# A re-planned head of an RMS norm and QKV projection: first tile cast and transposed in bfloat16, fourth tile loaded sooner, a crossbar transpose moved ahead of a weight piece

## The chip, the cores and the metric

One core of one Trainium2 chip. The metric is the device time of one execution in microseconds (us). "Span" is the time from the first to the last instruction of the profiled program; it is some 2 us shorter than the time. The calls ran on different chips, and each call ran the kernel before beside the others, so a ratio compares runs of one call.

## The reference

```python
batch, n_heads, seq, head_dim = 8, 12, 1024, 64          # x is 8192 x 768, w_qkv 768 x 2304
rms = np.sqrt(np.mean(x ** 2, axis=-1, keepdims=True) + eps)
x_norm = x / rms * gamma
return np.matmul(x_norm, w_qkv).astype(np.float32)
```

## The kernel before

64 row tiles of 128 rows. A tile is loaded in float32, turned into bfloat16 and transposed so that the 768 columns lie on the partitions (`xT`), and multiplied with `gamma * w_qkv` in bfloat16 (`w_b`). The row's 1/rms is applied as the product leaves PSUM. From the seventh tile on everything follows one regular loop. The first six tiles, the head, run while the weights arrive in pieces; there each operation stands in a hand-made list with a time that only sets the order of emission.

```python
HEAD = 6
def load_x(t):   X[t] = xin.tile(...);  nc.sync.dma_start(out=X[t], in_=xf[t*P:(t+1)*P, :])
def load_w(c):   # a float32 weight piece into one of (at most) 4 staging buffers of its shape
    WF[c] = wst.tile([P, k1-k0, n], f32, bufs=PIECE_BUFS[k1-k0, n]); nc.sync.dma_start(...)
def conv(c, ko, eng):  # w_b[:, ko, n0:n0+n] = WF[c] * gamma, on VectorE, ScalarE or GpSimd
def cast(t):     XB[t] = bfloat16 copy of X[t]
def stat(t):     # ScalarE: sum of squares, then sqrt
# three ways to the transposed tile xT:
def tr(t): ...        # six TensorE transposes of XB[t] in bfloat16 (L198), then cp(t): one copy out of PSUM
def tr_half(t, h): ...# TensorE transposes of X[t] in float32 (L212), 4 ("A") or 2 ("B"), then cp_half
def xbar(t):     nc.sync.dma_start_transpose(out=XT[t], in_=XB[t])   # crossbar transpose (L221)
def mm(t, n0, kos):    # products of tile t, 512 columns from n0, for these blocks of 128 (L234)
def idle(n, nl): ...   # products of zeros on TensorE while it waits (L286)

LOADS = [  # order on SyncE's queue: "w" a weight piece, "x" a tile, "t" a crossbar transpose
    w0, x0, x1, x2, w1, w2, w3, x3, w4, w5, w6, x4, w7, w8, w9, w10, x5, t4, w11, w12, w13, t5, w14, w15, x6, x7 ]
# [cut: the list HEAD_PLAN with its 166 entries, and the loop over tiles 6 to 63]
```

(The load list is abridged here to kinds and numbers.) Tiles 0, 1 and 2 are transposed on TensorE in float32, tile 3 in bfloat16, tiles 4 and 5 through the crossbar. `t5`, the crossbar transpose of the sixth tile, follows weight piece `w13`.

## Time and profile before

| | before |
|---|---|
| time, median of the first 3 runs | 388.32 us (387.97 to 388.36) |
| span of the profiled run | 386.2 us |
| TensorE busy | 98% |
| first product (L234) starts | 7.53 us |
| third tile landed | 7.78 us |
| sixth tile's crossbar transpose landed | 28.54 us |
| TensorE's wait for it | 0.33 us |
| first product of the seventh tile | 44.18 us |
| from there to the end of the span | 342.0 us |

How to read it: from 28.6 us TensorE has no hole until its last product, and from the seventh tile on nothing of the head is left. The lines that show this are in the prediction.

### The profile page before, as it was taken

What the parts mean: (1) busy time and instruction counts of PE and PEld (TensorE: products, weight loads), DVE (VectorE), ACT (ScalarE), POOL (GpSimd) and SP (SyncE); (2) the same over time, 40 slices, a digit from 0 to 9 for tenths busy, and PEclk for the clock granted to TensorE, in tenths of its full rate; (3) what the DMA queues carried; (4) which work ended last, traced back from release to release, by engine and by line L of the source; (5) the groups of instructions that cost most, each with busy time, mean ns of one, the idle gap of its engine ahead of it and who ended that gap; (6) DMA issues with size and microseconds to landing.
All of it is one profiled execution on the core that took longest, in us unless ns stands there. A gap on an engine that the chain in (4) does not pass through costs nothing.

```text
span 386.2 us, 5458 instructions
## 1 busy us (share of the span) xinstructions
PE 379.2 (98%) x1921; PEld 191.5 (50%) x1959; DVE 153.1 (40%) x307; ACT 181.5 (47%) x365; POOL 6.6 (2%) x14
## 2 busy tenths in 40 slices
PE   8999999999999999999999999999999999999996
PEld 4444655455454454554554554554554554554553
DVE  3744433433333344333344333343333343333332
ACT  5752644453544443544444444544444534444532
POOL 0130000000000000000000000000000000000000
PEclk9999999999999999999999999999999999999999
DMA  8999999999999999999999999999999999999995
GB/s 289 391 296 401 401 318 358 321 367 305 331 293 306 310 284 328 294 291 325 276 319 316 298 297 311 299 311 263 297 358 290 306 311 285 290 326 314 282 269 191
DMA packets 89575, 119.91 MB, mean 310 GB/s; under 512 B 52422, under 2 KB 61388, under 8 KB 89548
## 3 DMA queue, kind: packets, MB, share of 16 engines
q1 hardware_dynamic: 89536, 119.56, 101.5%
q8 instruction: 15, 0.25, 0.3%
q14 instruction: 12, 0.10, 0.1%
q10 hardware_dynamic: 12, 0.00, 0.0%
HBM read 32.25 MB, written 75.50 MB: 279 GB/s over the span
## 4 chain that ended last, share of the span: by engine, by line
PE 91%; DMA 6%; issue 1%; DVE 0%; ACT 0%; SPq 0%; DVEq 0%
PE pm L234 91%; DMA x_t<-in_x_dram 3%; DMA w_f<-in_w_qkv_dram 2%; DMA xT<-xb 2%; ACT ot L253 0%; DVE ot L251 0%; DVE xb L174 0%; SPq L160 0%; SPq L155 0%; DVEq L356 0%; ACT w_b L168 0%
## 5 line engine op out<-in xcount | busy, mean ns | idle before, releaser
L234 PE MATMUL pm<-w_b,xT 128*128 128x512 bf16 (+1 forms) x1882 | 372.1, 357 | 2.2 <-DMA xT<-xb 0.2
L234 PEld LDWEIGHTS <-xT 128*128 128x128 bf16 x1920 | 187.7, 98 | 185.6 <-DMA xT<-xb 0.7
L253 ACT ACTIVATE ot<-pm,rstd 128x512 f32<-128x512 f32 (+2 forms) x160 | 102.8, 644 | 192.3 <-PE pm L234 154.5
L251 DVE TENSOR_SCALAR ot<-pm,rstd 128x512 f32<-128x512 f32 (+1 forms) x161 | 111.3, 694 | 201.7 <-PE pm L234 199.1
L185 ACT ACTIVATE sq<-x_t 128x768 bf16<-128x768 f32 x64 | 53.3, 834 | 3.2 <-DMA x_t<-in_x_dram 3.2
L174 DVE CAST xb<-x_t 128x768 bf16<-128x768 f32 x61 | 33.2, 545 | 18.4 <-DMA x_t<-in_x_dram 18.2
L187 ACT ACTIVATE rms<-ssq,eps_sb 128x1 f32<-128x1 f32 x64 | 18.9, 295 | 2.1
L185 ACT ACTIVATION_READ_ACCUMULATOR sq<-x_t 128x1 f32 x64 | 12.2, 191 | 0.0
L166 DVE TENSOR_SCALAR w_b<-w_f,g_sb 128x512 bf16<-128x512 f32 (+1 forms) x16 | 7.7, 499 | 6.3 <-DMA w_f<-in_w_qkv_dram 6.3
L192 DVE RECIPROCAL rstd<-rms 128x1 f32<-128x1 f32 x64 | 9.8, 153 | 0.0
L170 POOL TENSOR_SCALAR w_b<-w_f,g_sb 128x512 bf16<-128x512 f32 (+1 forms) x8 | 5.9, 739 | 23.1 <-DMA w_f<-in_w_qkv_dram 23.1
L286 PE MATMUL pm<-const-float32-0.0 128*128 128x512 bf16 (+1 forms) x14 | 4.8, 491 | 0.8 <-PEq L342 0.8
L168 ACT ACTIVATE w_b<-w_f,g_sb 128x512 bf16<-128x512 f32 (+1 forms) x6 | 3.6, 612 | 2.9 <-DMA w_f<-in_w_qkv_dram 2.9
L212 PE MATMUL pm<-ident_f,x_t 128*128 128x128 f32 x18 | 2.6, 279 | 0.6 <-DMA x_t<-in_x_dram 0.5
L286 PEld LDWEIGHTS <-const-float32-0.0 128*128 128x128 bf16 x14 | 1.5, 123 | 2.6 <-issue 2.6
L212 PEld LDWEIGHTS pm<-ident_f,x_t 128*128 128x128 f32 x18 | 1.9, 140 | 1.6 <-DMA x_t<-in_x_dram 1.3
L176 ACT CAST xT<-pm 128x256 bf16<-128x256 f32 (+1 forms) x5 | 2.2, 454 | 0.2
L142 ACT ACT_TABLE_LOAD x1 | 1.3, 1283 | 1.4 <-PEq L342 1.4
L174 DVE CAST xT<-pm 128x512 bf16<-128x512 f32 x1 | 0.7, 690 | 0.7 <-PE pm L212 0.7
L269 DVE COPY g_sb<-pm 128x6 f32<-128x6 f32 x1 | 0.2, 165 | 1.7 <-PE pm L268 1.7
L268 PEld LDWEIGHTS pm<-ident_f,g 6*128 6x128 f32 x1 | 0.2, 177 | 0.8 <-issue 0.8
L174 DVE COPY xT<-pm 128x768 bf16<-128x768 bf16 x1 | 0.6, 557 | 0.0
(12 smaller groups left out, 2.5 us busy)
## 6 DMA issues: line engine op xcount, KB each, us to landing
out_dram<-ot SPq DMA_DIRECT2D x124, 512.0 KB, 3.9
x_t<-in_x_dram SPq DMA_DIRECT2D x64, 384.0 KB, 4.3
out_dram<-ot SPq DMA_DIRECT2D x64, 128.0 KB, 3.2
w_f<-in_w_qkv_dram SPq DMA_DIRECT2D x10, 512.0 KB, 7.5
out_dram<-ot SPq DMA_DIRECT2D x8, 256.0 KB, 2.0
w_f<-in_w_qkv_dram SPq DMA_DIRECT2D x4, 256.0 KB, 5.8
xT<-xb SPq DMA_TRANSPOSE x60, 4.3
w_f<-in_w_qkv_dram SPq DMA_DIRECT2D x2, 384.0 KB, 5.9
```

Source lines behind the costliest of these rows:

```text
L166: nc.vector.tensor_scalar(out=o, in0=i, scalar1=g, scalar2=None, op0=mult)
L168: nc.scalar.activation(out=o, in_=i, func=AF.Copy, scale=g, bias=0.0)
L170: nc.gpsimd.tensor_scalar(out=o, in0=i, scalar1=g, scalar2=1.0, op0=mult, op1=mult)
L174: nc.vector.tensor_copy(out=out, in_=in_)
L185: nc.scalar.activation(out=sq, in_=X[t], func=AF.Square, accum_out=ssq)
L187: nc.scalar.activation(out=rms, in_=ssq, func=AF.Sqrt, scale=inv_k, bias=eps_sb)
L192: nc.vector.reciprocal(out=r, in_=RS[t])
L212: nc.tensor.transpose(out=PT[t, h][:, ko - k0, :], in_=X[t][:, ko * P:(ko + 1) * P], identity=ident_f)
L234: nc.tensor.matmul(out=PM[t, n0][:, :nl], lhsT=XT[t][:, ko, :], rhs=w_b[:, ko, n0:n0 + nl], start=(b == 1), stop=(b == KO))
L251: nc.vector.tensor_scalar(out=o[:, :d], in0=pm[:, :d], scalar1=RS[t], scalar2=None, op0=mult)
L253: nc.scalar.activation(out=o[:, d:], in_=pm[:, d:nl], func=AF.Copy, scale=RS[t], bias=0.0)
L286: nc.tensor.matmul(out=wps[:, :nl], lhsT=zeros[:, :P], rhs=zeros[:, :nl], start=True, stop=True)
```

## The change

The intent: the head's list is planned anew. The first tile is cast and transposed in bfloat16 (the trace before has 0.057 us of TensorE for such a transpose, 0.108 us for one in float32); the fourth tile is loaded two pieces sooner, and the fifth one piece later; the third tile's transposes stand partly ahead of the first product; several conversions and evacuations change engines; the two crossbar transposes of the head come closer together (`t5` ahead of `w13`); the last weight columns are one piece, not two.

```diff
-          6, 1024, 512), (0, 2, 1536, 512), (2, 4, 1536, 512), (4, 6, 1536, 512), (0, 3, 2048,
-          256), (3, 6, 2048, 256)]
+          6, 1024, 512), (0, 2, 1536, 512), (2, 4, 1536, 512), (4, 6, 1536, 512), (0, 6, 2048,
+          256)]
 LOADS = [
-    (-8.95, "w", 2), (-8.94, "w", 3), (-8.93, "x", 3), (-8.92, "w", 4), (-8.91, "w", 5),
-    (-8.90, "w", 6), (-8.89, "x", 4), (-8.88, "w", 7), (-8.87, "w", 8), (-8.86, "w", 9),
-    (-8.85, "w", 10), (-8.84, "x", 5), (15.52, "t", 4), (15.53, "w", 11), (15.54, "w", 12),
-    (15.55, "w", 13), (22.65, "t", 5), (22.66, "w", 14), (22.67, "w", 15), (22.68, "x", 6),
-    (22.69, "x", 7),
+    (-8.95, "x", 3), (-8.94, "w", 2), (-8.93, "w", 3), (-8.92, "w", 4), (-8.91, "w", 5),
+    (-8.90, "w", 6), (-8.89, "w", 7), (-8.88, "x", 4), (-8.87, "w", 8), (-8.86, "w", 9),
+    (-8.85, "w", 10), (-8.84, "x", 5), (16.68, "t", 4), (16.69, "w", 11), (16.70, "w", 12),
+    (21.70, "t", 5), (21.71, "w", 13), (21.72, "w", 14), (21.73, "x", 6), (21.74, "x", 7),
 HEAD_PLAN = [
-    (4.98, "conv", 0, 0, "DVE"), (5.46, "conv", 0, 1, "DVE"), (5.94, "trA", 0), (5.98, "stat", 0),
-    (6.81, "trB", 0), (6.95, "cpA", 0, "DVE"), (7.03, "trB", 1), (7.24, "trA", 1),
-    (7.31, "cpB", 0, "ACT"), (7.63, "recip", 0), (7.67, "cpB", 1, "ACT"),
-    (7.69, "mm", 0, 0, "01"), (8.03, "cpA", 1, "ACT"), (8.12, "trB", 2), (8.34, "trA", 2),
-    [cut]
+    (4.98, "conv", 0, 0, "POOL"), (4.98, "conv", 0, 1, "ACT"), (5.98, "cast", 0, "DVE"),
+    (5.98, "stat", 0), (6.59, "tr", 0), (6.93, "trA", 1), (7.31, "cp", 0, "ACT"),
+    (7.37, "recip", 0), (7.37, "trB", 1), (7.53, "cpA", 1, "DVE"), (7.93, "trA", 2),
+    (8.16, "stat", 2), (8.36, "mm", 0, 0, "01"), (8.50, "cpA", 2, "DVE"),
+    [cut: the rest of the list]
-    at(2.81, idle, 6, NT)
+    at(2.81, idle, 8, NT)
```

## The prediction

> **What bounds the kernel now.** I read the page first (busy shares, then the chain that ended last), then TensorE's own timeline over the first 60 us, then the chain in order of time, the queue of SyncE, and a table of windows around the one wait that was left.
>
> ```profile
> PE 379.2 (98%) x1921; PEld 191.5 (50%) x1959; DVE 153.1 (40%) x307; ACT 181.5 (47%) x365; POOL 6.6 (2%) x14
> ...
> PE 91%; DMA 6%; issue 1%; DVE 0%; ACT 0%; SPq 0%; DVEq 0%
> ```
>
> TensorE is busy for 98% of the span and carries 91% of the chain; the rest of the chain is the first loads. The change touches only the head (six row tiles computed while the weights arrive), so what matters is how much time TensorE spends there on anything but the product. Its timeline (start us, us, what):
>
> ```profile
> 3.19 2.16 PE L286 MATMUL pm<-const-float32-0.0 128*128 128x512 bf16 x6
> 5.84 1.85 PE L212 MATMUL pm<-ident_f,x_t 128*128 128x128 f32 x12 [0.49 <-DMA x_t<-in_x_dram]
> 7.53 0.59 PE L234 MATMUL pm<-w_b,xT 128*128 128x512 bf16 x2
> 7.97 0.82 PE L212 MATMUL pm<-ident_f,x_t 128*128 128x128 f32 x6
> 8.62 2.97 PE L234 MATMUL pm<-w_b,xT 128*128 128x512 bf16 x13
> 11.46 0.51 PE L198 MATMUL pm<-ident,xb 128*128 128x128 bf16 x6
> 11.81 0.34 PE L286 MATMUL pm<-const-float32-0.0 128*128 128x128 bf16 x3
> 12.06 16.35 PE L234 MATMUL pm<-w_b,xT 128*128 128x512 bf16 x73
> 28.58 31.75 PE L234 MATMUL pm<-w_b,xT 128*128 128x512 bf16 x167 [0.17 <-DMA xT<-xb]
> ```
>
> Only starts count here, since the ends are modelled. Products of width 512 start 0.216 us apart. From 12.06 to 28.03 us there is no hole (two records are missing, each leaving exactly double the spacing), and from 28.58 us to the last product at 382.5 us none either. So the head before loses: everything until 7.53 us; 0.65 us for the third tile's six float32 transposes (7.97 to 8.62); 0.63 us for the fourth tile (the product before it would have ended at 11.43, the next starts at 12.06: six bfloat16 transposes, three idle products and about 0.1 us of waiting); 0.33 us at 28.25 for the sixth tile's crossbar transpose. That last one is where the chain enters TensorE for good:
>
> ```profile
> 22.19 6.35 DMA xT<-xb
> ...
> 28.58 6.00 PE pm L234 x27
> ```
>
> Check of the account: six tiles are 6 x 27 = 162 products of width 512. The products of the 58 later tiles run from 44.18 us to 382.61 us, 338.43 / 1566 = 0.2161 us each. So 7.53 + 162 x 0.2161 + 0.65 + 0.63 + 0.33 = 44.15 us against the 44.18 us at which the seventh tile starts. From there to the end it is 342.0 us of span, with no wait, so the change moves the total by what it moves this one start.
>
> Why the crossbar transpose came late (window, length, PE busy, clock, DMA share, GB/s):
>
> ```profile
> 25.50:26.20 0.70, 0.70 (x5) 1.00 1.15 314
> 26.20:27.60 1.40, 1.40 (x8) 1.00 1.57 32
> ```
>
> For 1.4 us the DMA engines moved 32 GB/s while their packets stayed open. In the trace's packets, 23 of this transpose's 256-byte packets each lasted 1.43 to 1.46 us and all ended at 27.67 to 27.71 us. One engine had been held back by a 16,384-byte instruction packet (22.25 to 23.34 us); my reading is that the transpose waits for the engine that is furthest behind.
>
> **What the Trainium skill says.** "TensorE: Matmul & The Clock Gate", section "What's actually happening", has the clock fall to half only after about 3.4 us of idleness, and rise after as long a busy stretch. The trace agrees: idle products started 0.427 us apart until 4.45 us, then 0.22, and the lull from about 5.2 to 7.53 us did not bring the slow spacing back. "Runtime: NRT & Kernel Launch", section "Terms", says instruction memory is refilled in 16 KiB blocks; the trace shows such packets (15 on queue 8, 0.25 MB). "Advanced Engine Details and Errata", section "X-Bar Transpose (TRN2)", calls transpose DMAs as fast as regular ones; the 32 GB/s window disagrees for a transpose behind a lagging engine. "SBUF — State Buffer", section "Who interferes with whom", has GpSimd and a VectorE operation in a two-port mode shut each other out for a whole instruction; a weight conversion on VectorE took 0.80 us at 13.20 beside one of GpSimd that began at 13.03, against a median of 0.49.
>
> **The change part by part.** Durations from the groups by shape and the spacing of starts:
>
> ```profile
> L212 PE MATMUL pm<-ident_f,x_t 128*128 128x128 f32 x18 | 2.6, 279 | 0.6 <-DMA x_t<-in_x_dram 0.5
> ...
> L176 ACT CAST xT<-pm 128x512 bf16<-128x512 f32 x2 | 1.2, 586 | 0.1
> L176 ACT CAST xT<-pm 128x256 bf16<-128x256 f32 x3 | 1.1, 366 | 0.1
> ...
> L198 PE MATMUL pm<-ident,xb 128*128 128x128 bf16 x6 | 0.5, 221 | 0.0
> ```
>
> A float32 transpose takes 0.108 us of TensorE (starts 6.01, 6.12, 6.23), a bfloat16 one 0.057 (11.53, 11.59, 11.64).
>
> *First tile.* Its data landed at 5.80 us. The cast on VectorE takes 0.56 us (5.84 to 6.40), six bfloat16 transposes 0.34 us (6.44 to 6.79). The copy goes to ScalarE after the statistics, which ended at 7.08; from 0.586 us at 512 columns and 0.366 at 256 I estimate 0.81 us at 768, so done at 7.9. VectorE no longer converts the first two weight pieces; GpSimd and ScalarE do, 0.69 and 0.72 us from 4.87, both finished before the cast begins.
>
> *Second and third tile.* Second: landed 6.78, transposes 6.82 to 7.48. Third: landed 7.78, four transposes 7.82 to 8.26. They now stand ahead of the first product, which therefore starts at 8.26 and not 7.53 us: **+0.73**. The later two (0.22 us) stay inside the stream, where six stood: 0.22 - 0.65 = **-0.43**.
>
> *Fourth tile.* Loaded two 256 KB pieces sooner, each 0.67 us at the rate of the trace, hence at about 9.4 us in place of 10.82. Cast on VectorE by 10.1 (behind the two half copies, 8.46 to 9.15 and to 9.5), and the stream reaches its transposes at about 10.2 with products left over to cover the copy. The three idle products and the wait go: 0.35 - 0.63 = **-0.28**. The pieces pushed back land at about 10.1 and 10.8; their products come at 10.8 and 12.3. The one converted by GpSimd (landed 8.44, done about 9.2, 9.5 if shut out) is needed at 9.77.
>
> *Crossbar transposes.* The one for the sixth tile still waits for the cast at 22.2 us, but one 512 KB weight piece that went before it now comes after it. Pieces landed at 25.12, 26.47 and 27.86, the transpose 0.68 us after the last. With one fewer I expect about 27.1 us, wanted at about 28.2: **-0.33**. The pieces behind it are first needed at 37 us or later, ten us of slack, and the joined last piece carries the same bytes as the two that it replaces.
>
> *Moved evacuations.* Both engines have room (40% and 47% busy), and I followed the eight accumulator buffers in order of allocation: the closest is the first tile's first evacuation, done about 14.4, its buffer wanted at 14.9. Nothing here is on the path. The extra two idle products end near 5.6 us, in time that waited for data anyway.
>
> Sum: 0.73 - 0.43 - 0.28 - 0.33 = -0.31 us. Seventh tile at about 43.87 us, and 388.32 - 0.31 = **388.0 us**.
>
> **The rivals.** (1) *The crossbar wait stays or grows.* For it: the instruction refill comes at a count of instructions which hardly changes, and with the two transposes close together the second may meet the same laggard sooner; if it lands as late as before, the gain is gone (388.3), and one us later gives 389.3. Against it: 1.1 us of slack from the dropped piece. (2) *The early stream starves.* The fourth tile, the GpSimd conversion and the half copies have 0.1 to 0.6 us of slack each; a miss passes on only its excess, say 0.2 to 0.4 us, giving 388.2 to 388.4. (3) *The clock falls back* in the longer lull of products, now 5.6 to 8.26 us = 2.6 us; if transposes did not keep it awake and a window fell inside, products at 0.43 us for some 3 us would cost about 1.6 us: 389.6. Against: 2.6 is under 3.4. (4) *Everything that starts late is made up elsewhere*, so that a gap appears which I don't see; the stream is dense, so there is nothing to hide in.
>
> **Range and chances.** The three runs before spread over 0.39 us, as large as the expected gain. Crossbar slack on one side, small misses and another chip on the other: 387.4 to 388.7 us should hold it 8 times in 10. Two per cent would be 7.8 us; the whole head before the first product is 7.5 us, so faster by 2% is all but impossible (0.005). Slower by 2% needs a failure far beyond the rivals (0.01). Within: 0.985.
>
> **What would show it.** First product near 8.26 us; third tile's remaining transposes 0.22 us in the stream; fourth tile's near 10.2 with no wait after; the sixth tile's crossbar transpose landing before 28 us and no wait of TensorE for it; seventh tile starting at 43.7 to 44.0; from there 342.0 us as before. I'd be wrong if new waits on a conversion or a copy stand between 8 and 14 us, if the chain still enters TensorE through a crossbar transpose, or if half-speed spacing shows after 8 us.

## The result, and the profile after

The changed kernel took 388.09 us, median of 6 runs (387.80 to 389.01), the kernel before 388.25 (387.97 to 388.36, 6 runs). The ratio is 1.0, with a 95% interval of 0.9987 to 1.0012. (Ratios are the mean time of one kernel's runs over that of the other's of the same rounds, so not quite the ratio of the medians.) The two are the same: no gain in time is clear of the noise, and what the change did has to be read from the traces. The time lies in the predicted range, 0.09 us from the predicted value. The range (387.4 to 388.7) holds the time before as well, so lying in it says little about the account behind it.

The page of the changed kernel, busy shares and the chain that ended last:

```profile
PE 379.7 (98%) x1920; PEld 191.7 (50%) x1958; DVE 155.3 (40%) x311; ACT 178.2 (46%) x357; POOL 9.3 (2%) x18
...
PE 98%; issue 1%; DVE 0%; ACT 0%
```

The 6% of DMA that stood in the chain before are gone: the chain stays on TensorE down to the start. (The chain misses that the first product still hangs on the third tile's load, as the table of starts below shows: the wait for that load is short, and the ends of TensorE's instructions are modelled.) Its timeline from 3.35 to 60 us (start us, us, what), to be laid beside that of before:

```profile
3.35 3.59 PE L286 MATMUL pm<-const-float32-0.0 128*128 128x512 bf16 x8
6.73 0.59 PE L198 MATMUL pm<-ident,xb 128*128 128x128 bf16 x6
7.16 1.43 PE L212 MATMUL pm<-ident_f,x_t 128*128 128x128 f32 x10
8.42 1.03 PE L234 MATMUL pm<-w_b,xT 128*128 128x512 bf16 x4
9.29 0.38 PE L212 MATMUL pm<-ident_f,x_t 128*128 128x128 f32 x2
9.51 1.03 PE L234 MATMUL pm<-w_b,xT 128*128 128x512 bf16 x4
10.37 0.50 PE L198 MATMUL pm<-ident,xb 128*128 128x128 bf16 x6
10.70 49.65 PE L234 MATMUL pm<-w_b,xT 128*128 128x512 bf16 x248
```

The first product starts at 8.42 us, later than the 7.53 of before. After that only 0.22 us (third tile, 9.29 to 9.51) and 0.33 us (fourth tile, 10.37 to 10.70) are not products, and from 10.70 us there is no hole at all: the wait at 28 us is gone. The seventh tile starts at 43.99 us instead of 44.18, and the span ends 341.97 us later, as before.

Three things in this profile were not foreseen. First, the stall of the DMA engines at the sixth tile's crossbar transpose is still there (window, length, PE busy, clock, DMA share, GB/s), only no longer on the path:

```profile
25.40:26.80 1.40, 1.40 (x8) 1.00 1.26 44
26.80:27.70 0.90, 0.90 (x6) 1.00 1.12 322
```

Second, a new thin stretch of DMA traffic, where the kernel before moved 389 and 391 GB/s:

```profile
16.50:17.00 0.50, 0.50 (x4) 1.00 1.09 307
17.00:18.00 1.00, 1.00 (x6) 1.00 0.79 199
```

SyncE's own waits up to 20 us say why:

```profile
SPq L160 <- DMA w_f<-in_w_qkv_dram: 4.3, 1, 4.3
...
SPq L160 <- POOL w_b L170: 1.4, 1, 1.4
```

SyncE stood for 5.7 us (4.3 + 1.4) with the tenth weight piece in hand and issued it only at 15.76 us, just after GpSimd's second conversion of the seventh piece ended at 15.73. The buffer addresses of the compiled program (no profile shows them) agree: before, the tenth piece got the sixth's staging buffer, now it gets the seventh's, which is free later.

Third, the slow clock of TensorE (idle products 0.427 us apart) lasted here until 6.73 us, in the kernel before until 4.45 us. So the eight idle products ended near 6.7 us, where the prediction had 5.6, and the first tile's copy began at 7.36 us where it began at 6.95 in a second profile (e7; 0.17 us of this is a later landing). It was done at 8.16, still ahead of the third tile's transposes, which ended just before 8.42.

### The profile page after: what moved, and what is told of

Same layout as the page of the kernel before. It is cut to its first block, busy times and chain, and to the rows that moved or that the text cites. A ratio compares the mean times of both kernels' runs of the same rounds, so it can differ in the third digit from the quotient of the medians.

```text
span 386.0 us, 5446 instructions
## 1 busy us (share of the span) xinstructions
PE 379.7 (98%) x1920; PEld 191.7 (50%) x1958; DVE 155.3 (40%) x311; ACT 178.2 (46%) x357; POOL 9.3 (2%) x18
## 4 chain that ended last, share of the span: by engine, by line
PE 98%; issue 1%; DVE 0%; ACT 0%
PE pm L234 96%; PE pm L286 2%; PE pm L212 0%; DVE ot L251 0%; PE pm L198 0%; ACT ot L253 0%; PE pm L268 0%
## 5 line engine op out<-in xcount | busy, mean ns | idle before, releaser
L251 DVE TENSOR_SCALAR ot<-pm,rstd 128x512 f32<-128x512 f32 (+1 forms) x167 | 114.5, 691 | 195.5 <-PE pm L234 194.9
L253 ACT ACTIVATE ot<-pm,rstd 128x512 f32<-128x512 f32 (+2 forms) x154 | 99.1, 646 | 191.8 <-PE pm L234 147.6
L170 POOL TENSOR_SCALAR w_b<-w_f,g_sb 128x512 bf16<-128x512 f32 (+1 forms) x12 | 8.6, 719 | 23.3 <-DMA w_f<-in_w_qkv_dram 23.3
L168 ACT ACTIVATE w_b<-w_f,g_sb 128x512 bf16<-128x512 f32 (+1 forms) x7 | 4.7, 689 | 6.3 <-DMA w_f<-in_w_qkv_dram 6.2
L286 PE MATMUL pm<-const-float32-0.0 128*128 128x512 bf16 x13 | 5.9, 628 | 0.8 <-PEq L342 0.8
L166 DVE TENSOR_SCALAR w_b<-w_f,g_sb 128x512 bf16<-128x512 f32 (+1 forms) x11 | 4.8, 457 | 2.3 <-DMA w_f<-in_w_qkv_dram 2.3
L174 DVE CAST xT<-pm 128x512 bf16<-128x512 f32 (+1 forms) x3 | 1.7, 599 | 0.5 <-PE pm L212 0.4
L212 PE MATMUL pm<-ident_f,x_t 128*128 128x128 f32 x12 | 1.8, 278 | 0.0
L198 PEld LDWEIGHTS <-xb 128*128 128x128 bf16 x12 | 0.9, 106 | 0.8 <-DVE xb L174 0.5
L198 PE MATMUL pm<-ident,xb 128*128 128x128 bf16 x12 | 1.1, 230 | 0.0
```

What stands on the lines that cost most here:

```text
L166: nc.vector.tensor_scalar(out=o, in0=i, scalar1=g, scalar2=None, op0=mult)
L168: nc.scalar.activation(out=o, in_=i, func=AF.Copy, scale=g, bias=0.0)
L170: nc.gpsimd.tensor_scalar(out=o, in0=i, scalar1=g, scalar2=1.0, op0=mult, op1=mult)
L174: nc.vector.tensor_copy(out=out, in_=in_)
L212: nc.tensor.transpose(out=PT[t, h][:, ko - k0, :], in_=X[t][:, ko * P:(ko + 1) * P], identity=ident_f)
L251: nc.vector.tensor_scalar(out=o[:, :d], in0=pm[:, :d], scalar1=RS[t], scalar2=None, op0=mult)
```

## The experiments

My theory after the result: the account of the prediction holds, so the seventh tile's start is the sum of four terms, and the whole gain comes from the crossbar transpose, since the other three add up to nothing (0.73 - 0.43 - 0.28 = 0.02). The rivals: the reordered head itself (bfloat16 transposes, sooner fourth tile) is what gains; the DMA hole costs something; the clock decides. To compare profiles, one fact helps: the moment at which the first loads land differs from run to run by up to 0.6 us (third tile: 7.70 to 8.28 us), and all the head of the changed kernel shifts with it. So the fourth column of numbers, seventh tile less third tile's landing, is the one to read. It is left out for the kernels before, whose first product does not wait for the third tile.

| kernel | third tile landed | first product | seventh tile | difference | mean span (runs) |
|---|---|---|---|---|---|
| changed, profile 1 | 7.89 | 8.42 | 43.99 | 36.10 | 386.05 (6) |
| changed, profile 2 (e7) | 7.72 | 8.26 | 43.83 | 36.11 | 385.84 (5) |
| changed, profile 3 (e11) | 7.98 | 8.52 | 44.08 | 36.10 | 386.20 (5) |
| t5 behind w13 again (e2) | 8.28 | 8.82 | 44.87 | 36.59 | 386.92 (5) |
| first tile float32 (e3) | 7.70 | 8.23 | 43.80 | 36.10 | 385.98 (5) |
| six staging buffers (e4) | 7.86 | 8.40 | 43.96 | 36.10 | 386.04 (5) |
| instruction packet sooner (e5) | 7.77 | 8.31 | 44.77 | 37.00 | 386.62 (4) |
| six idle products (e6) | 7.89 | 8.43 | 43.99 | 36.10 | 386.08 (5) |
| first product sooner (e10) | 7.86 | 7.63 | 43.94 | 36.08 | 385.88 (5) |
| one VectorE instruction more (e12) | 7.75 | 8.29 | 43.85 | 36.10 | 386.16 (5) |
| before | 7.78 | 7.53 | 44.18 | | 386.29 (9) |
| before, t5 ahead of w13 (e1) | 7.75 | 7.53 | 43.79 | | 385.98 (5) |
| the same again (e9) | 7.75 | 7.52 | 44.26 | | 386.22 (5) |
| before, fourth tile sooner (e8) | 8.14 | 7.89 | 44.69 | | 386.80 (4) |

### e1: only the crossbar transpose moved, in the kernel before

```diff
-    (15.55, "w", 13), (22.65, "t", 5), (22.66, "w", 14), ...
+    (22.65, "t", 5), (22.655, "w", 13), (22.66, "w", 14), ...
```

> The kernel before with one line of the load order changed: the sixth tile's crossbar transpose is issued ahead of the fourteenth weight piece instead of behind it. My account (the transpose lands one piece after the other, so one piece fewer ahead of it brings it 0.7 to 1.3 us sooner): it lands at about 27.2 to 27.8 us instead of 28.54, TensorE's wait of 0.33 us at 28.25 goes, and the seventh tile starts at 43.8 to 43.9 instead of 44.18; time about 0.3 us less than before, near 387.9. Rival (the transpose is held by the DMA engine that fetched instructions, whatever stands ahead of it): it still lands at 28.3 or later, the wait stays, no change of time. Second rival (the piece pushed back becomes the new wait): a wait of VectorE or ScalarE for that piece, and a hole in TensorE between 29 and 34 us.

Measured: the transpose landed at 27.20 us, the wait is gone, the seventh tile started at 43.79 us. Time 387.76 us (387.73 to 388.29), ratio to before 0.9991 (0.9978 to 1.0003). TensorE's timeline:

```profile
11.77 0.34 PE L286 MATMUL pm<-const-float32-0.0 128*128 128x128 bf16 x3
12.02 48.35 PE L234 MATMUL pm<-w_b,xT 128*128 128x512 bf16 x247
```

Where the kernel before broke at 28.25 us, one run of products now goes on from 12.02 us. This one line of the load order takes 0.39 us off the seventh tile's start, as much as the whole change did in its best profile (43.83). The first rival falls for this profile; e9, below, takes up whether it always goes so.

### e2: only the crossbar transpose moved back, in the changed kernel

```diff
+    (16.71, "w", 13), (21.70, "t", 5), (21.72, "w", 14), ...
-    (21.70, "t", 5), (21.71, "w", 13), (21.72, "w", 14), ...
```

> The changed kernel with that one part undone: the fourteenth weight piece is loaded ahead of the sixth tile's crossbar transpose again. My account: the transpose lands at about 29.1 us (the piece at 28.4, then 0.7), is wanted at 28.43, so TensorE waits about 0.7 us where it waited for nothing, and the seventh tile starts at 44.6 to 44.8; time 0.5 to 0.8 us more than the changed kernel, near 388.7. Rival (the transpose's place in the queue does not matter): seventh tile still at 44.0, no wait.

Measured: landed at 29.23 us; 389.06 us (388.94 to 389.23), ratio 1.0021 (1.0007 to 1.0035), about 1 us over the changed kernel.

```profile
11.10 17.86 PE L234 MATMUL pm<-w_b,xT 128*128 128x512 bf16 x82
29.27 31.10 PE L234 MATMUL pm<-w_b,xT 128*128 128x512 bf16 x167 [0.31 <-DMA xT<-xb]
```

By starts, the hole before 29.27 us is 0.47 us (28.58 to 29.27 less one product of 0.22), and the difference column says the same, 36.59 - 36.10 = 0.49. The rest of the later start, 0.4 us, is that the first loads landed late in this profile. But all five runs have spans of 386.8 to 387.1, and the profiled one is among the shortest, so something of that size stood in every run of this program; whether the swap brings it is not shown. So the place of this transpose in the queue counts in both kernels; the size, foretold as 0.7, was 0.5, and the time came out about 0.35 us over the 388.7 foretold.

### e3: the first tile in float32 again, in the changed kernel

```diff
-    (5.98, "cast", 0, "DVE"), ... (6.59, "tr", 0), ... (7.31, "cp", 0, "ACT"),
+    (5.98, "trA", 0), (5.99, "trB", 0), ... (7.30, "cpA", 0, "DVE"), (7.31, "cpB", 0, "ACT"),
```

> The changed kernel with the first tile transposed in float32 again, as before (no cast; the two halves copied by VectorE and ScalarE); all else as changed. My account: the first product is held by the third tile's landing (7.89 us) and its four transposes, so the first tile's way is worth next to nothing by itself: first product at 8.4 to 8.5, seventh tile at 44.0 to 44.1, time within 0.1 us of the changed kernel. Rival (the bfloat16 transposes of the first tile are what saves the time, 6 x 0.05 = 0.3 us): seventh tile 0.3 us later or more, time 388.4 or more.

Measured: 387.96 us (387.91 to 388.52), ratio 0.9996 (0.9983 to 1.0008); difference 36.10 us, to the hundredth that of the changed kernel.

```profile
5.79 2.61 PE L212 MATMUL pm<-ident_f,x_t 128*128 128x128 f32 x16
8.23 1.03 PE L234 MATMUL pm<-w_b,xT 128*128 128x512 bf16 x4
```

All 16 float32 transposes are through before 8.23 us, the last four after the third tile's landing at 7.70. What the bfloat16 form saves for the first tile is TensorE time in which it would wait for the third tile anyway. The part of the change with which its short description begins is worth nothing here.

### e4: six staging buffers instead of four, in the changed kernel

```diff
-    PIECE_BUFS = {(k1 - k0, n): min(4, sum(...
+    PIECE_BUFS = {(k1 - k0, n): min(6, sum(...
```

> The changed kernel with six staging buffers for the 512 KB weight pieces in place of four, because its trace shows SyncE blocked from 10.2 to 15.7 us on a buffer and the DMA engines half idle from 16.5 to 18.0 us. My account: that hole lies off the path, as the pieces and transposes behind it had 0.7 us of slack; the tenth piece is issued near 10 us, the hole goes, the sixth tile's data land near 21.6 instead of 22.08, its transpose near 27.3 instead of 27.69, and neither the seventh tile (44.0) nor the time moves (within 0.1 us). Rival (the hole costs time further on): seventh tile or the end 0.3 us sooner, near 387.7.

Measured: the hole in the DMA traffic is gone,

```profile
17.00:18.00 1.00, 1.00 (x6) 1.00 1.04 385
```

the sixth tile landed at 21.66 us (22.08 before it), its transpose at 27.16 (27.69), and nothing came of it: difference 36.10, 388.08 us (387.98 to 388.81), ratio 0.9998 (0.9985 to 1.0010). The hole was real and off the path. (How much sooner the transpose lands without it is less sure: with four buffers it landed at 27.64 to 27.74 in the three profiles of the changed kernel, but at 27.39 to 27.50 in e3, e6, e10 and e12.)

### e5: the instruction packet 26 TensorE instructions sooner, in the changed kernel

```diff
-    at(0.0, idle, 5, NT)
+    at(0.0, idle, 10, NT // 2)
-    at(2.81, idle, 8, NT)
+    at(2.81, idle, 16, NT // 2)
```

> The changed kernel with its 13 idle products of width 512 made into 26 of width 256: the same idle time, 26 TensorE instructions more, so that the 16 KiB instruction packet that fell at 22.2 us comes about 2.8 us sooner, ahead of the fifth tile's crossbar transpose instead of behind it. My reading (a transpose waits for the DMA engine that is furthest behind): the stall of 1.3 us moves from the sixth tile's transpose (25.5 to 26.8 us) to the fifth tile's (near 21.5), which lands at about 24 instead of 22.99 and is wanted at 23.83, so TensorE waits 0.1 to 0.4 us for it; seventh tile at 44.1 to 44.4, time 0.1 to 0.4 us more. Rival (the stall belongs to the second of two transposes close together): a window of under 50 GB/s stays at 25.5 to 26.8 us and the fifth tile's transpose lands at 23.0 as before.

Measured: the 16,384-byte packet came at 18.34 us instead of 22.16. The stall moved as expected from the sixth tile's transpose to the fifth's:

```profile
21.60:23.00 1.40, 1.15 (x6) 1.00 0.93 38
23.00:24.00 1.00, 1.00 (x6) 1.00 1.03 299
25.40:26.80 1.40, 1.40 (x8) 1.00 1.12 326
```

The fifth tile's transpose landed at 24.07 us (22.99). But TensorE's wait was longer than expected and for something else:

```profile
21.85 38.42 PE L234 MATMUL pm<-w_b,xT 128*128 128x512 bf16 x201 [0.73 <-DVE w_b L166]
```

By starts it is 0.90 us, just the 37.00 - 36.10 of the difference column. It waited for a conversion of the tenth weight piece, which landed at 20.89 us where it had landed at 19.62: the piece itself was late before any transpose was. From 20.5 to 21.8 us the trace's packets of the weight pieces (2,048 bytes) ended one at a time, some 84 ns apart, where 176 had ended from 19.0 to 20.0 us: I read this as one of the 16 DMA engines still at its share, while the others had gone on to the next load. 388.84 us (388.47 to 389.02), ratio 1.0015 (1.0002 to 1.0029). So the rival (the second of two transposes stalls as such) is out, my reading of who is waited for fits, and I had overlooked that the packet delays plain loads too. The packets of the other stalls bear the reading out: in one microsecond of each, only 11 or 12 such load packets ended (12 in the kernel before from 26.4 us, 11 in the changed one from 25.6, 12 in e1 from 25.0), where 185 ended in e1 from 23.0 and 191 in the changed kernel from 24.0. That is the share of one engine in 16, while transpose packets stood open.

### e6: six idle products instead of eight, in the changed kernel

```diff
-    at(2.81, idle, 8, NT)
+    at(2.81, idle, 6, NT)
```

> The changed kernel with six idle products after gamma instead of eight, as before. The trace of the changed kernel showed the slow clock (starts 0.427 us apart) until 6.7 us, that of the kernel before until 4.45 us, so the moment of waking varies from run to run. Theory one (the two more idle products guard against products at the slow clock): with six, TensorE is less busy from 5.9 to 8.4 us, in some runs the clock wakes later and the products after 8.4 us start 0.43 us apart for a while; median 0.1 to 0.5 us more and a wider spread, with single runs near 389. Theory two[...]: first product at 8.4, same time as changed within 0.1 us.

Measured: 388.09 us (388.01 to 388.51), ratio 1.0001 (0.9988 to 1.0015), difference 36.10 us. Theory two: six suffice as well. No profile showed products at the slow spacing, though the idle products and first transposes kept it until 4.0 us in one (e11) and 6.7 us in another (changed, profile 1). The two added idle products changed nothing that these runs can see.

### e7 and e11: the changed kernel again, twice

> The changed kernel itself once more, for its size against before and as the reference of the other experiments: 0.1 to 0.3 us under the kernel before (0.19 us by the starts of the seventh tile, about 0.3 once the 0.12 us by which all of its first loads landed later in that profile are taken off). If the run of 389.01 us was chance, no more than one of the runs here is over 388.6; if the changed schedule has a second, slower course, several are.

> The changed kernel a third time, as partner of the runs before and after it in this list, and for the odd long run (389.01 once in eleven so far): 387.9 to 388.1 median. If the long run belongs to the schedule, another over 388.7 among these five; else none. The seventh tile starts 36.1 us after the third tile's data have landed (36.10 and 36.11 in the two profiles so far), whatever the landing.

Measured: e7 387.98 us (387.86 to 388.20), ratio 0.9995 (0.9983 to 1.0008); e11 388.19 us (387.84 to 388.90), ratio 1.0002 (0.9990 to 1.0015). e7 is the prediction's case nearly to the letter: first product 8.26 us, seventh tile 43.83. But e11 had two odd runs (388.81 and 388.90; spans 386.7 and 386.8), so with 389.01 there are 3 in 16; the kernel before has none in its 36 runs of these four calls, all between 387.92 and 388.54. Of the variants, e4 has one too (388.81, span 386.7), and e8 an outlier of its own (389.80, span 387.8). The odd runs have the span of e5 (386.3 to 386.9), where the instruction packet came ahead of the fifth tile's transpose. That would fit, but none of the odd runs was the profiled one, so it stays open.

### e8: only the fourth tile sooner, in the kernel before

```diff
-    (-8.95, "w", 2), (-8.94, "w", 3), (-8.93, "x", 3), (-8.92, "w", 4)
+    (-8.95, "x", 3), (-8.94, "w", 2), (-8.93, "w", 3), (-8.92, "w", 4)
```

> The kernel before with only the load order of the fourth tile changed: it comes two 256 KB pieces sooner, while TensorE's order stays. My account: the two pieces pushed back land about 1.0 us later (10.2 and 10.8 us), the products that need the first of them at 10.13 us find it converted at about 10.75, so a new wait of 0.5 to 0.6 us opens there, and about 0.1 us of waiting at the fourth tile's own place goes: seventh tile at 44.5 to 44.7, time 0.3 to 0.6 us more than before. Rival (the earlier load of the fourth tile by itself is a gain): seventh tile at 44.1 or sooner.

Measured: 388.52 us (388.23 to 389.80), ratio 1.0015 (1.0000 to 1.0030); seventh tile at 44.69.

```profile
8.98 1.67 PE L234 MATMUL pm<-w_b,xT 128*128 128x512 bf16 x7
11.05 1.52 PE L234 MATMUL pm<-w_b,xT 128*128 128x512 bf16 x6 [0.40 <-DVE w_b L166]
```

The new wait is there, 0.56 us by starts, for the piece pushed back. But the 44.69 is right by luck: 0.36 us of it is that the second tile landed late in this profile (7.13 us), so that the first product started at 7.89. The rest is 0.16 us: 0.56 lost here and 0.06 in a small second wait, 0.13 won at the fourth tile's place, and the 0.33 us wait at 28 us swallowed, because TensorE now reaches it later than the transpose (28.80 us) lands. I had left that last term out. A delay ahead of a wait is free up to the length of the wait.

### e9: e1 once more

> The kernel before with the sixth tile's transpose ahead of the fourteenth weight piece, once more, now beside the changed kernel on one chip. If all of the gain is that one line, it is as fast as the changed kernel: medians within 0.15 us of one another, seventh tile at 43.7 to 43.9. If the reordered head adds something of its own, the changed kernel is faster by 0.2 us or more.

Measured: 388.18 us (387.99 to 388.28) beside e11's 388.19, ratio to before 0.9997 (0.9983 to 1.0010). As fast as the changed kernel, but by luck: e11 had two odd runs, and here the seventh tile started at 44.26, outside what was foretold and no sooner than in the kernel before.

```profile
12.01 11.60 PE L234 MATMUL pm<-w_b,xT 128*128 128x512 bf16 x51
23.92 36.28 PE L234 MATMUL pm<-w_b,xT 128*128 128x512 bf16 x188 [0.31 <-DMA xT<-xb]
```

The same program now waited at 23.23 to 23.92 us for the fifth tile's transpose, which landed at 23.87 instead of 22.38. Windows of e1 first, then of e9:

```profile
22.00:23.00 1.00, 1.00 (x6) 1.00 0.91 336
...
24.80:26.20 1.40, 1.40 (x8) 1.00 1.29 41
```

```profile
22.00:23.00 1.00, 1.00 (x6) 1.00 0.05 5
...
24.80:26.20 1.40, 1.40 (x8) 1.00 1.05 355
```

In e1 the instruction packet started at 21.81 us and the stall fell on the sixth tile's transpose; in e9 it started at 21.44 us, while the fifth tile's transpose was moving, and the stall fell there. A third of a microsecond decides which transpose is hit, in one and the same program. The packets of e9 show who waited: 15 packets of the next load stood open from 21.8 to 21.9 us until 23.35 to 23.43, while, after the instruction packet had ended at 22.53, the last 13 packets of the transpose ended one after another (22.56 to 22.93). The spans of e1's runs show both courses (three of 385.8, then 386.2 and 386.3), those of e9 only the longer one (386.1 to 386.3). Over both, the one line takes some 0.2 us off the mean span (386.10 against 386.29), and the wait that it removes can come back at the fifth tile.

### e10: the first product ahead of the third tile's transposes, in the changed kernel

```diff
-    (6.93, "trA", 1), (7.31, "cp", 0, "ACT"), ... (7.93, "trA", 2), ... (8.36, "mm", 0, 0, "01"),
+    (6.93, "trA", 1), (6.94, "cph", 0, "A", "DVE"), (7.31, "cph", 0, "B", "ACT"), ...
+    (7.92, "mm", 0, 0, "01"), (7.93, "trA", 2),          # cph: cp for blocks 0-3 or 4-5 alone
```

> The changed kernel with its one idle stretch of TensorE filled, which the account points to: it stands idle between the second tile's transposes and the third tile's landing (about 0.3 us). The first tile's copy is split, its first four blocks on VectorE, and the first tile's first two products stand ahead of the third tile's transposes. My account: first product at 7.4 to 7.6 in place of 8.3, the two products (0.43 us) use 0.2 to 0.3 us that was idle, and the later waits for conversions at 10 to 11 us take back up to 0.1; seventh tile 35.8 to 35.95 us after the third tile's landing in place of 36.1, time 0.15 to 0.3 us under the changed kernel, near 387.75. Rival (the stream is held by the pieces' landings, not by this hole): new waits of 0.2 to 0.3 us between 9 and 13 us, seventh tile at 36.1 us after the landing again.

Measured: 387.66 us (387.49 to 387.84), ratio to before 0.9985 (0.9972 to 0.9997), the lowest, and no run above the fastest of e11 on the same chip. Yet my account of it fell:

```profile
8.49 0.59 PE L239 MATMUL pm<-w_b,xT 128*128 128x512 bf16 x2
8.93 0.38 PE L217 MATMUL pm<-ident_f,x_t 128*128 128x128 f32 x2
9.45 1.04 PE L239 MATMUL pm<-w_b,xT 128*128 128x512 bf16 x4
```

The first product did start at 7.63 us, but between 9.15 and 9.45 us TensorE now waits 0.30 us for the copy of the third tile, whose transposes came later. The seventh tile starts 36.08 us after the landing, 0.02 sooner. The rival had it right, and the time foretold (387.75) was met for another reason. The span is that of the changed kernel's good runs; what fell is the time outside the span: 1.78 us, where the changed kernel has 2.15.

### e12: one more VectorE instruction, in the changed kernel

Time less span (each span is rounded to 0.1 us) was 1.89 to 2.08 us in the runs of the kernel before (mean 1.97), 2.09 to 2.20 in all 16 of the changed kernel (mean 2.15), 1.95 and 1.93 on average in e1 and e9. The compiled programs have 440 VectorE instructions in the kernel before, 442 in the changed one, 443 in e10.

```diff
     nc.vector.memset(eps_sb, float(eps))
+    more = singles.tile([P, 1], f32)
+    nc.vector.memset(more, float(eps))
```

> The changed kernel with one more VectorE instruction (a memset of 128x1 that nothing reads), 443 in place of 442, as in the run whose first product came sooner. The time less the span was 2.15 us in every run of the changed kernel, 1.96 in those of the kernel before and 1.78 in that run, so part of what the change gains in the span is lost outside of it. Theory one (the length of VectorE's program sets it): 1.75 to 1.85 us here, the span as changed (385.7 to 386.0, odd runs 386.8), time near 387.65. Theory two (it goes with something else in the program): 2.1 to 2.2 us, time near 388.0. An odd run of over 386.5 us of span is again to be expected in about one of five, if those belong to the changed schedule.

Measured: time less span 1.76 to 1.82 us in all five runs (mean 1.79). One instruction that nothing uses takes 0.36 us off the time outside the span. Theory one, as far as it goes: one VectorE instruction more moves it. (e12 also adds a tile of 128x1; e10 adds none and has 1.78.) TensorE's count does not seem to: 13 products more in e5 and two fewer in e6 leave it at 2.17 and 2.13. By which rule (440 gives 1.97, 441 in e2 and 442 give 2.14 and 2.15, 443 gives 1.78 and 1.79), no run tells, and the first of these also differs on the other engines. 387.96 us (387.61 to 388.30), ratio 0.9996 (0.9982 to 1.0010): the good runs were at 387.6 as foretold, but the spans again had long ones (386.5 twice, 386.2), so the median gained little.

## Why the prediction was right

- *First product, +0.73 us to 8.26.* In e7, where the third tile landed 0.06 us sooner than in the kernel before, it was 8.26; in the first profile 8.42, with a landing 0.11 us later. In these traces it is the landing plus 0.53 or 0.54 us, where I had 0.48, so the exact 8.26 of e7 is luck: a sooner landing made up for a sum too small. Whatever the landing does, the gain follows: the seventh tile's start moved by -0.35 (e7), -0.19 (first profile) and -0.10 us (e11, at 44.08, outside the 43.7 to 44.0 foretold). The copy of the first tile on ScalarE, estimated as 0.81 us, took 0.798.
- *Third tile, -0.43.* Exact: 0.22 us in the stream (9.29 to 9.51) for 0.65.
- *Fourth tile, -0.28.* 0.33 us at 10.37 us and no wait after it, so -0.30.
- *Crossbar transpose, -0.33.* The wait went in all profiles of the changed kernel, and e1 and e2 show by doing and undoing that this step is worth 0.4 to 0.5 us of the start, as much as the whole gain. e9 sets a limit: there the same step left the start where it was, because the stall fell on the fifth tile's transpose instead. That the other three terms cancel is read from the traces; of them only the first tile's form (e3) and the first product's place (e10) were undone in the changed kernel. The landing was mis-sized: 27.1 foretold, 27.64 to 27.74 measured, because I carried over the landings of the trace before, in which the tenth piece waited for the sixth piece's buffer. It got the seventh's, SyncE stood still, and the DMA engines ran thin; e4 without that gives 27.16, though part of the difference may be chance (27.39 to 27.50 in e3, e6, e10 and e12, which had it too). I also left out that the fifth tile is loaded one piece later: its transpose landed at 22.99 us in place of 22.35, still in time. The slack of 1.1 us shrank to some 0.7 and sufficed.
- *The sum.* 0.73 - 0.43 - 0.30 - 0.33 = -0.33; e7 against the kernel before: 43.83 - 44.18 = -0.35.
- *From the start of the seventh tile to the time.* Half right: the 342.0 us of span held in every profile that I compared. But I subtracted the gain from the time as if the time outside the span stood still. It grew by 0.18 us. Over its 16 runs the changed kernel's mean span is 386.03 us against some 386.3 before, a gain of about 0.25 with three odd runs in it, of which the time keeps less than 0.1.
- *Moved evacuations, idle products, clock.* No wait of the stream on any of them; in e6 two idle products fewer had no effect. The rival of the falling clock did not occur. The rival of a stall at the second transpose did, off the path; e5 and e9 show that such a stall can come onto it, at the first of the two or by way of a weight piece. Two readings of the prediction need a correction. The 6% of DMA in the chain before were not only the first loads: 1.6% was the sixth tile's crossbar transpose itself. And the conversion of 0.80 us beside one of GpSimd shows a slowdown, not a whole block: one begun only after GpSimd's had ended (13.72) would have ended 1.01 us after 13.20, at the median of 0.49.

## What to carry to other kernels

Where the bounding engine is dense after the head, write its head as a sum of starts and holes, and ask of each part of a plan which term it moves: here a long re-plan had three terms that cancel, and one swapped pair of loads was worth as much as all of it. Look for the last wait on the path before anything else, and remember that delays ahead of it are free up to its length. Differences of a few tenths of a microsecond are not to be read off times alone: compare starts within traces, relative to a landing, and check the time outside the span.

## What the Trainium skill lacked or had wrong

- "Runtime: NRT & Kernel Launch", section "Instruction fetch mechanics", calls the cost of crossing a 16 KiB block mostly hidden. Here such a packet lasted 1.0 to 1.2 us, and what shared the DMA engines with it came late (a weight piece at 20.89 instead of 19.62 us in e5), for up to 0.90 us of TensorE. Moving it by 26 instructions moved the damage.
- "Advanced Engine Details and Errata", section "X-Bar Transpose (TRN2)", speaks of the rate of transpose DMAs and of two transposing streams at once, not of a transpose beside ordinary loads that lag. That a crossbar transpose stands open on the other engines until the one furthest behind has come up, with 38 to 44 GB/s moving for 1.4 us in e5 and the changed kernel, is not there. The packets agree: during the stall one engine's share of load packets ended (11 or 12 in a microsecond, of some 190), and nearly nothing else.
- "TensorE: Matmul & The Clock Gate", section "What you observe", gives the moment of waking as about 4 us of sustained products, with 500 ns from run to run. Here the slow spacing ended between 4.0 us (e11) and 6.7 us (changed, profile 1), with the first idle product at 0.77 us each time and a pause of some 0.3 to 0.5 us near 3 us: 3.2 to 6.0 us after it, a wider spread than that sentence gives. (The next section of the page itself lets the number of slow products differ more from run to run.)
- No page has it that one VectorE instruction more can shorten the time outside the profiled span, by 0.36 us (2.15 to 1.79) in e12.
